# Two fused blocks on one core: four pieces of small work change their place around the last expert

## Chip, cores and metric

The kernel runs on one core of one Trainium2 chip. The metric is the device time of one execution in microseconds (us). Engines are named as in the profile: PE is TensorE (PEld its weight loads), DVE VectorE, ACT ScalarE, POOL GpSimd, SP SyncE. Each engine works through its own queue in order; semaphores let one wait for another.

## What is computed

Two blocks in a row on 512 tokens of width 1024. The first is differential attention, followed by a mixture of 16 experts in 4 groups, with two experts chosen for each token:

```python
h = silu(xt @ w_gate[e]) * (xt @ w_up[e])
h = h * combine[..., e]
y = y + h @ w_down[e]
```

The second block normalises the tokens and a context of 256 rows, shifts and scales both by factors made from a condition, projects them with one matrix, and mixes a Fourier branch with neighbourhood attention, in which every token also attends to the context:

```python
xn = _rms_norm(x, norm_g) * (1.0 + sc_x) + sh_x
cn = _rms_norm(ctx, norm_g) * (1.0 + sc_c) + sh_c
qx = _rms_norm(_heads(qx), q_norm_g)
kc = _rms_norm(_heads(kc), k_norm_g)
```

## The kernel before

Every float32 operand of a matmul is held as two float16 parts, high and low, and every product is three matmuls (`mm3`: high by high, high by low, low by high). `hilo` makes the parts: ACT writes the high one, DVE the low one. For a weight, `Weights.piece()` does this for 1024 of the 2048 columns of a buffer at a time; a weight matrix has four pieces. Its raw form is loaded by DMAs of 1 MB on SP's queue.

The experts come one after the other: `pick` gathers an expert's (up to 96) tokens by a one-hot matmul (`se`, `xgp`), `hidden` is the gate or up projection (bank `gu`), `silu` and `gated` make `hx` = silu(gate) * up, `down` is the projection back (bank `yp`), which ACT copies to `y` and POOL's queue stores to `y_d`. The one-hot matrices need each token's rank within its expert; the ranks come from router logits (`lgp`, `lgq`), a handful of tiny DVE operations (`ranks`, tile `misc_m`) and a counting matmul (`pk`).

Most of the program is ordered by a scheduler, which may move an instruction ahead of where it is written. From the last but one expert (`tail`, a manual schedule) to the second block's first projections the written order holds. The names of that stretch:

- `crow`, the two context row tiles (buffer `ctx`). Line 1101 takes their reciprocal norms (`row_rstd`: a Square with row sums on ACT, a tiny multiply-add on DVE, a power on POOL); line 1103 multiplies the rows by them on DVE.
- `W["k"]`, the key weights (raw `bk`, parts `bks`), and `W["v"]`, the value weights (`bv`, `bvs`). Before, one piece of the key weights stands behind the up projection of expert 15 and three behind the first two context columns.
- `spread` (line 1107 for the scale, `aB`; line 1243 for the shift, `bB`) spreads a row of factors over 128 partitions by 8 matmuls into each of two PSUM banks, which ACT copies to `AB`.
- After `down(15)` each engine reads a flag and may branch to a path for overfull experts (lines 1110 and 1111). Then `fetch` gathers each token's two expert rows from `y_d` by 8 indirect DMAs on POOL's queue (`yg`), `combined(t)` adds them to the token rows `XQ` by two DVE operations of 1024 columns for each of the four row tiles.
- `context_cols(k)` transposes 128 columns of the context on PE (`cnp`), and ACT and DVE make `cnT`; `project_c` projects keys (`kc`) and values (`vc`) of the context.
- `row_scale`, `row_affine`, `row_flip`: norm, scale and shift, transpose (`xnp`) of the four token row tiles. `row_affine` multiplies by scale and norm on DVE and adds the shift (line 1213), on POOL for row tiles 0 and 2 and on DVE for 1 and 3. The transposed rows `xnT` feed the keys `kx` (96 matmuls), and then `vx`, `qx` and `ng`, which PE runs one after the other.
- Lines 1289 to 1292 load the gains of the query and key norms (`g2rows`) over the router's weights in tile `sm` and multiply them by two DVE operations of 64 columns. They stand behind the manual schedule, so the scheduler places them.

Of the kernel before, what the change touches and what calls it, by code (L numbers as in the profile page):

```python
# [14 lines left out]
ALU = mybir.AluOpType  # L15
# [6 lines left out]
D = 1024  # L22
NT = 4
KD = 8
EPS = 1e-6
# [75 lines left out]
def block_kernel(ctx: ExitStack, tc: tile.TileContext, a, out, dbg=None):  # L101
    nc = tc.nc
# [100 lines left out]
    def rsqrt(ss, n, mult, eps, name):  # L203
        u = tiny.tile([P, n], F32, tag=f"rs{n}", name=name + "u")
        nc.vector.tensor_scalar(u, ss, mult, eps, op0=ALU.mult, op1=ALU.add)
        r = tiny.tile([P, n], F32, tag=f"rr{n}", name=name + "r")
        nc.gpsimd.tensor_tensor(r, u, mhalf[:, :n], op=ALU.pow)
        return r

    def row_rstd(src, name, scale=1.0):  # L210
        ss = tiny.tile([P, 1], F32, tag="ss", name=name + "ss")
        junk = sqt(name + "j").bitcast(F16)
        nc.scalar.activation(junk, src, AF.Square, accum_out=ss)
        return rsqrt(ss, 1, 1.0 / (D * scale * scale), EPS / (scale * scale), name)

    def transpose_to(o, in_, n=P):
# [147 lines left out]
    W = {}  # L364
# [604 lines left out]
    def hidden(e, j, nxt):  # L969
        wh, wl = EW[3 * e + j].w  # L970
        h, l = xgs[e]
        ps = bank("mm", f"gu{j}_{e}")
        for m in range(4):
            ms = slice(m * P, (m + 1) * P)
            o = ps[:, m * CAP:(m + 1) * CAP]
            for k in range(KD):
                mm(o, wh[:, k, ms], h[:, k, :], k == 0, False)
                mm(o, wh[:, k, ms], l[:, k, :], False, False)
                mm(o, wl[:, k, ms], h[:, k, :], False, k == KD - 1)
            if nxt:  # L980
                nxt.piece()
        psg[e, j] = ps
# [6 lines left out]
    def gated(e):  # L989
        sg = ht[e]  # L990
        stt(sg[:, :W4], psg[e, 1][:, :W4], DG * HS, sg[:, :W4], op1=ALU.mult)
        hx = h15(f"hx{e}")
        hilo(hx[:, :W4], hx[:, W4:], sg[:, :W4])
        ht[e] = hx
# [86 lines left out]
    e = NE - 2  # L1081
# [6 lines left out]
    crow, AB = ([x[:, i * D:(i + 1) * D] for i in range(2)] for x in (slot("ctx"), slot("AB")))  # L1088
    for t in range(2):
        nc.sync.dma_start(crow[t], a["ctx"][t * P:(t + 1) * P, :])  # L1090
    gated(e)
    e = NE - 1
    hidden(e, 0, EW[3 * e + 1])
# [4 lines left out]
    XP = rows("XQ")  # L1098
    for t in range(NT):
        nc.sync.dma_start(XP[:, t, :], x1_d[t * P:(t + 1) * P, :])  # L1100
    crs = [row_rstd(crow[t], f"cn{t}") for t in range(2)]
    for t in range(2):
        nc.vector.tensor_scalar(crow[t], crow[t], crs[t], None, op0=ALU.mult)
    hidden(e, 1, None)
    W["k"].piece(1)
    gated(e)
    run_all(spread(lambda k: aff[:, 0, k:k + 1], AB[0], "aB"))
    down(e, None)

    most = nc.values_load(flag[0:1, 0:1], min_val=0, max_val=2 * T)  # L1110
    with tc.If(most > CAP):
# [98 lines left out]
    def row_affine(t):  # L1210
        x = w4(f"xr{t}")
        stt(x, XP[:, t, :], rr[t], AB[0], op1=ALU.mult)
        (nc.gpsimd if t in (0, 2) else nc.vector).tensor_tensor(x, x, AB[1], op=ALU.add)
        xr[t] = x

    def row_flip(t):
# [22 lines left out]
        fetch(t)  # L1239
    context_cols(0)  # L1240
    context_cols(1)
    W["k"].piece(3)
    run_all(spread(lambda k: mod[:, k, 0:1], AB[1], "bB"))
    for k in range(KD):
        for t in range(2):
# [30 lines left out]
    for t, f in enumerate(kcn):  # L1276
        turn(f, cnat[:, t * 512:(t + 1) * 512], csp[:, t * 1024:(t + 1) * 1024],
             kvc16[:, :2048].rearrange("p (m t) -> p m t", m=8)[:, :, t * P:(t + 1) * P])()
    maskb = const.tile([P, 1152], F32, tag="misc", name="misc_b")
    mask = maskb[:, :768]  # L1280
    nc.sync.dma_start(mask, a["mask"])
# [4 lines left out]
    load_bias(0)  # L1286
    tail.close()

    nc.gpsimd.dma_start(S("wr", 0, 128), a["g2rows"])
    g2r = S("wr", 0, 64)  # L1290
    nc.vector.tensor_tensor(g2r, g2r, S("wr", 64, 64), op=ALU.mult)
    nc.vector.tensor_scalar(g2r, g2r, 4.0, None, op0=ALU.mult)
    gxc = const.tile([P, KD], F32, name="gxc")
    nc.vector.tensor_scalar(gxc, mod[:, 16:24, 0], 1.0 / (4.0 * SW), None, op0=ALU.mult)
    nc.gpsimd.dma_start(gx_d[0, :].rearrange("(k p) -> p k", p=P), gxc)
# [321 lines left out]
```

## Time and profile before

| | us |
|---|---|
| median of three runs | 856.88 |
| lowest, highest | 855.62, 859.67 |
| the profiled execution | 857.49 |
| span of its profile | 855.7 |

| engine | busy us | share of the span |
|---|---|---|
| PE | 788.8 | 92% |
| PEld | 495.6 | 58% |
| DVE | 642.0 | 75% |
| ACT | 522.0 | 61% |
| POOL | 148.7 | 17% |

Times below are counted from the start of the span; the profiled execution is 1.8 us longer than its span. The router stands at 270 to 300 us, the experts at 295 to 577, the context's projections at 577 to 606, the token rows and their keys at 594 to 636; from there to 699 PE runs without a gap. PE's clock has two levels, 2.4 GHz (1.00 in the profile) and 1.2 GHz (0.50); the mean granted was 0.979.

### The profile page before, as it was taken

The numbers are of one execution on the slowest core, as the hardware profiler recorded it, in microseconds if no ns is written. First come the engines' busy times: TensorE is split into PE (matmuls) and PEld (weight loads), VectorE is DVE, ScalarE is ACT, GpSimd is POOL, SyncE is SP. The second block draws the span as 40 slices with busy tenths as digits, with TensorE's granted clock in tenths as the row PEclk, the third lists the DMA queues.
The fourth block names the chain that finished last, engine by engine and source line by source line (L and its number), as shares of the span: only waits on it lengthen the run. The fifth ranks groups of instructions, "written<-read, shape, count | busy, mean of one in ns | idle before, by whom it ended". The sixth has DMA issues, their size and how long they took to land. (4 is left out here: it accounts for less than half of the span.)

```text
span 855.7 us, 18940 instructions
## 1 busy us (share of the span) xinstructions
PE 788.8 (92%) x7898; PEld 495.6 (58%) x7898; DVE 642.0 (75%) x1114; ACT 522.0 (61%) x847; POOL 148.7 (17%) x132
## 2 busy tenths in 40 slices
PE   5999999898989889999999999988899999899598
PEld 3445445454446588888888787754444445645344
DVE  4756658578985688999999999957955638986642
ACT  5635346455854378888887888767434347789400
POOL 1140121110053310000000000005550313231000
PEclk9999999999999799999999999999999999999899
DMA  9944201594163959999999999956554129696912
GB/s 339 388 169 148 99 1 26 161 266 164 50 242 128 333 193 350 393 394 398 395 395 396 397 395 394 367 194 230 189 164 138 30 57 199 137 200 126 252 59 68
DMA packets 127257, 192.91 MB, mean 225 GB/s; under 512 B 56271, under 2 KB 56784, under 8 KB 127168
## 3 DMA queue, kind: packets, MB, share of 16 engines
q1 hardware_dynamic: 121184, 172.33, 60.6%
q0 software_dynamic: 3776, 13.05, 4.2%
q10 hardware_dynamic: 2208, 6.29, 1.9%
q8 instruction: 63, 1.03, 0.5%
q14 instruction: 26, 0.21, 0.1%
HBM read 165.95 MB, written 12.59 MB: 209 GB/s over the span
## 5 line engine op out<-in xcount | busy, mean ns | idle before, releaser
L155 PEld LDWEIGHTS <-hT 128*128 128x128 f16 x576 | 55.8, 100 | 66.9 <-issue 9.9
L155 PEld LDWEIGHTS <-xnT 128*128 128x128 f16 x456 | 44.5, 99 | 53.6 <-issue 2.4
L155 PEld LDWEIGHTS <-hx 128*96 128x96 f16 x384 | 46.5, 125 | 39.7 <-ACT hx L166 5.5
L525 ACT ACTIVATE z<-z,mx 128x128 f32<-128x128 f32 (+3 forms) x64 | 35.4, 555 | 37.0 <-DVE mx L523 34.4
L1009 POOL DMA_DIRECT2D y_d<-y x16 | 8.2, 513 | 256.5 <-ACT y L1008 245.4
L155 PE MATMUL xgp<-se,XSh 128*128 128x96 f16 x512 | 48.3, 211 | 0.9 <-DVE se L940 0.9
L155 PE MATMUL xgp<-se,XSl 128*128 128x96 f16 x512 | 48.3, 211 | 0.0
L155 PEld LDWEIGHTS <-XSl 128*128 128x128 f16 x512 | 45.6, 101 | 1.0 <-issue 1.0
L155 PEld LDWEIGHTS <-XSh 128*128 128x128 f16 x512 | 45.6, 101 | 0.7 <-issue 0.7
L155 PEld LDWEIGHTS <-cT 128*128 128x128 f16 x216 | 20.4, 101 | 23.5 <-issue 4.3
L523 DVE CUSTOM_DVE_ANT_0 z<-s,misc_a 128x128 f32<-128x128 f32 (+3 forms) x64 | 29.8, 483 | 5.1 <-PE s L155 5.1
L1481 POOL TENSOR_TENSOR late_b<-late_b,misc_b 128x256 f32<-128x256 f32 x24 | 19.1, 818 | 78.8 <-DVE mxn L1484 74.6
L163 DVE SCALAR_TENSOR_TENSOR ring<-zn,ring 128x512 f16<-128x512 f32 x32 | 21.7, 699 | 13.7 <-ACT ring L1487 13.7
L155 PEld LDWEIGHTS <-oT 128*128 128x128 f16 x192 | 17.4, 99 | 20.8 <-issue 4.1
L1486 ACT ACTIVATE zn<-zn,mxn 128x512 f32<-128x512 f32 x32 | 22.8, 714 | 10.5 <-DVE mxn L1484 10.3
L155 PE MATMUL y<-wo0s,oT 128*128 128x512 f16 x96 | 26.5, 381 | 1.4 <-DVE on L577 1.2
L1484 DVE CUSTOM_DVE_ANT_0 zn<-ns,late_b 128x512 f32<-128x512 f32 x32 | 20.8, 679 | 8.1 <-PE ns L155 8.1
L155 PE MATMUL y<-wo1s,oT 128*128 128x512 f16 x96 | 23.9, 390 | 3.0 <-DVE XP L163 2.2
L1008 ACT ACTIVATE y<-yp 96x512 f32<-96x512 f32 x32 | 18.7, 586 | 9.1 <-PE yp L155 9.1
L155 PE MATMUL s<-kk,qk 64*128 64x128 f16 (+3 forms) x192 | 24.0, 302 | 0.2 <-DVE mx L523 0.2
L155 PE MATMUL v<-wv1s,hT 128*128 128x512 f16 x96 | 23.9, 399 | 0.0
L155 PE MATMUL z<-bo0s,cT 128*128 128x512 f16 x96 | 22.8, 384 | 1.1 <-DVE fg L163 1.1
(731 smaller groups left out, 2338.9 us busy)
## 6 DMA issues: line engine op xcount, KB each, us to landing
w_gate<-in_w_gate SPq DMA_DIRECT2D x32, 1024.0 KB, 13.2
w_up<-in_w_up SPq DMA_DIRECT2D x32, 1024.0 KB, 13.2
w_down<-in_w_down SPq DMA_DIRECT2D x32, 1024.0 KB, 13.5
ada<-in_w_ada SPq DMA_DIRECT2D x12, 1024.0 KB, 7.0
y_d<-y POOLq DMA_DIRECT2D x16, 384.0 KB, 7.2
wk<-in_da_w_in SPq DMA_DIRECT2D x4, 1024.0 KB, 13.5
wv<-in_da_w_in SPq DMA_DIRECT2D x4, 1024.0 KB, 10.8
wo<-in_da_w_out SPq DMA_DIRECT2D x4, 1024.0 KB, 10.2
```

The lines of the kernel that those rows point to most:

```text
L155: nc.tensor.matmul(o, lhsT=lhsT, rhs=rhs, start=start, stop=stop)
L163: return nc.vector.scalar_tensor_tensor(o, in0, sc, in1, op0=op0, op1=op1)
L523: nc.vector.tensor_tensor_reduce(out=z[:, :n], in0=ps[:, :n], in1=master[:, 384 - P * i:], scale=-hsc, scalar=3e38, op0=ALU.add, op1=ALU.m ...
L525: nc.scalar.activation(z[:, :n], z[:, :n], AF.Exp, bias=mx, scale=-1.0, accum_out=sums[:, c, i:i + 1])
L1008: nc.scalar.activation(y[:CAP, cs], ps[:CAP, :], AF.Copy, scale=1.0 / (HS * SW))
L1009: nc.gpsimd.dma_start(y_d[e * CAP:(e + 1) * CAP, :], y[:CAP, :])
L1481: nc.gpsimd.tensor_tensor(m[:, :256], pos[j, "b"][:, c * 256:(c + 1) * 256], mask[:, v:v + 256], op=ALU.add)
L1484: nc.vector.tensor_tensor_reduce(out=z, in0=st[j, t][c], in1=m, scale=-ISC, scalar=3e38, op0=ALU.add, op1=ALU.min, accum_out=mx)
L1486: nc.scalar.activation(z, z, AF.Exp, bias=mx, scale=-1.0, accum_out=sums[:, 2 * t + c:2 * t + c + 1])
```

## The change

Five edits, all of them of order or of engine; the arithmetic is the same.

1. The gating of expert 15 (`gated(e)`) stands ahead of the tiny operations and multiplies of the context's norm, of which only the two Squares on ACT (`row_squares`) stay ahead of it.
2. The key weights' four pieces all stand around and within `down(15)`: one ahead of it, two behind its first bank's matmuls, one behind its second's. Before, `down(15)` had none.
3. The shift of all four row tiles is added by DVE.
4. The load of the gains stands behind the context's load on SP's queue, in place of POOL's.
5. Their two multiplies stand at the end of the manual schedule, behind the norms of the context's keys.

```diff
--- before.py
+++ after.py
@@ -207,10 +207,14 @@
         nc.gpsimd.tensor_tensor(r, u, mhalf[:, :n], op=ALU.pow)
         return r
 
-    def row_rstd(src, name, scale=1.0):
+    def row_squares(src, name):
         ss = tiny.tile([P, 1], F32, tag="ss", name=name + "ss")
         junk = sqt(name + "j").bitcast(F16)
         nc.scalar.activation(junk, src, AF.Square, accum_out=ss)
+        return ss
+
+    def row_rstd(src, name, scale=1.0):
+        ss = row_squares(src, name)
         return rsqrt(ss, 1, 1.0 / (D * scale * scale), EPS / (scale * scale), name)
 
     def transpose_to(o, in_, n=P):
@@ -1088,6 +1092,7 @@
     crow, AB = ([x[:, i * D:(i + 1) * D] for i in range(2)] for x in (slot("ctx"), slot("AB")))
     for t in range(2):
         nc.sync.dma_start(crow[t], a["ctx"][t * P:(t + 1) * P, :])
+    nc.sync.dma_start(S("wr", 0, 128), a["g2rows"])
     gated(e)
     e = NE - 1
     hidden(e, 0, EW[3 * e + 1])
@@ -1098,14 +1103,15 @@
     XP = rows("XQ")
     for t in range(NT):
         nc.sync.dma_start(XP[:, t, :], x1_d[t * P:(t + 1) * P, :])
-    crs = [row_rstd(crow[t], f"cn{t}") for t in range(2)]
+    css = [row_squares(crow[t], f"cn{t}") for t in range(2)]
+    hidden(e, 1, None)
+    gated(e)
+    crs = [rsqrt(css[t], 1, 1.0 / D, EPS, f"cn{t}") for t in range(2)]
     for t in range(2):
         nc.vector.tensor_scalar(crow[t], crow[t], crs[t], None, op0=ALU.mult)
-    hidden(e, 1, None)
+    run_all(spread(lambda k: aff[:, 0, k:k + 1], AB[0], "aB"))
     W["k"].piece(1)
-    gated(e)
-    run_all(spread(lambda k: aff[:, 0, k:k + 1], AB[0], "aB"))
-    down(e, None)
+    down(e, W["k"])
 
     most = nc.values_load(flag[0:1, 0:1], min_val=0, max_val=2 * T)
     with tc.If(most > CAP):
@@ -1210,7 +1216,7 @@
     def row_affine(t):
         x = w4(f"xr{t}")
         stt(x, XP[:, t, :], rr[t], AB[0], op1=ALU.mult)
-        (nc.gpsimd if t in (0, 2) else nc.vector).tensor_tensor(x, x, AB[1], op=ALU.add)
+        nc.vector.tensor_tensor(x, x, AB[1], op=ALU.add)
         xr[t] = x
 
     def row_flip(t):
@@ -1239,7 +1245,6 @@
         fetch(t)
     context_cols(0)
     context_cols(1)
-    W["k"].piece(3)
     run_all(spread(lambda k: mod[:, k, 0:1], AB[1], "bB"))
     for k in range(KD):
         for t in range(2):
@@ -1276,6 +1281,9 @@
     for t, f in enumerate(kcn):
         turn(f, cnat[:, t * 512:(t + 1) * 512], csp[:, t * 1024:(t + 1) * 1024],
              kvc16[:, :2048].rearrange("p (m t) -> p m t", m=8)[:, :, t * P:(t + 1) * P])()
+    g2r = S("wr", 0, 64)
+    nc.vector.tensor_tensor(g2r, g2r, S("wr", 64, 64), op=ALU.mult)
+    nc.vector.tensor_scalar(g2r, g2r, 4.0, None, op0=ALU.mult)
     maskb = const.tile([P, 1152], F32, tag="misc", name="misc_b")
     mask = maskb[:, :768]
     nc.sync.dma_start(mask, a["mask"])
@@ -1286,10 +1294,6 @@
     load_bias(0)
     tail.close()
 
-    nc.gpsimd.dma_start(S("wr", 0, 128), a["g2rows"])
-    g2r = S("wr", 0, 64)
-    nc.vector.tensor_tensor(g2r, g2r, S("wr", 64, 64), op=ALU.mult)
-    nc.vector.tensor_scalar(g2r, g2r, 4.0, None, op0=ALU.mult)
     gxc = const.tile([P, KD], F32, name="gxc")
     nc.vector.tensor_scalar(gxc, mod[:, 16:24, 0], 1.0 / (4.0 * SW), None, op0=ALU.mult)
     nc.gpsimd.dma_start(gx_d[0, :].rearrange("(k p) -> p k", p=P), gxc)
```

The three stretches of the queues. First DVE's queue in the router, before: `lgq` is the last row tile's logits, `sm` the gains, `ge` to `misc_m` the ranks, `pk` the counts, `se` the first expert's one-hot matrix.

```order
L163 SCALAR_TENSOR_TENSOR misc_m<-lgq,m3r,sm 128x20
L1291 TENSOR_TENSOR sm<-sm 128x64
L873 TENSOR_TENSOR ge<-misc_m 128x80
L1292 TENSOR_SCALAR sm<-sm 128x64
L875 TENSOR_TENSOR ge<-ge,cst 128x80
L876 TENSOR_TENSOR df<-ge 128x20x4
L877 TENSOR_REDUCE misc_m<-df 128x20
L163 SCALAR_TENSOR_TENSOR misc_m<-misc_m 128x16
L163 SCALAR_TENSOR_TENSOR misc_m<-misc_m,pk 128x64
L940 TENSOR_TENSOR se_3084<-misc_m,cst 128x384
```

The same rows of the changed kernel:

```order
L163 SCALAR_TENSOR_TENSOR misc_m<-lgq,m3r,sm 128x20
L877 TENSOR_TENSOR ge<-misc_m 128x80
L879 TENSOR_TENSOR ge<-ge,cst 128x80
L880 TENSOR_TENSOR df<-ge 128x20x4
L881 TENSOR_REDUCE misc_m<-df 128x20
L163 SCALAR_TENSOR_TENSOR misc_m<-misc_m 128x16
L163 SCALAR_TENSOR_TENSOR misc_m<-misc_m,pk 128x64
L944 TENSOR_TENSOR se_3084<-misc_m,cst 128x384
```

The two operations on `sm` have left the router; in the changed kernel they stand far behind, between the sums of the token keys' norms.

DVE's queue ahead of expert 15's down projection, before (`sg` and `hx` are the gating, `cn0u`, `cn1u` and `ctx` the context's norm, `bks` the key weights):

```order
L163 SCALAR_TENSOR_TENSOR w_down15s_8486<-w_down_7995,w_down15s_8486 128x1024 x2
L205 TENSOR_SCALAR cn0u<-cn0ss 128x1
L205 TENSOR_SCALAR cn1u<-cn1ss 128x1
L1103 TENSOR_SCALAR ctx<-ctx,cn0r 128x1024
L1103 TENSOR_SCALAR ctx<-ctx,cn1r 128x1024
L163 SCALAR_TENSOR_TENSOR bks_8616<-bk_8449,bks_8616 128x1024
L163 SCALAR_TENSOR_TENSOR sg_8447<-gu_15_8519,sg_8447 128x384
L168 TENSOR_TENSOR hx_8620<-sg_8447,hx_8620 128x384
L1110 TENSOR_LOAD misc_m
```

And in the changed kernel:

```order
L163 SCALAR_TENSOR_TENSOR w_down15s_8487<-w_down_7995,w_down15s_8487 128x1024 x2
L163 SCALAR_TENSOR_TENSOR sg_8448<-gu_15_8510,sg_8448 128x384
L168 TENSOR_TENSOR hx_8608<-sg_8448,hx_8608 128x384
L205 TENSOR_SCALAR cn0u<-cn0ss 128x1
L205 TENSOR_SCALAR cn1u<-cn1ss 128x1
L1111 TENSOR_SCALAR ctx<-ctx,cn0r 128x1024
L1111 TENSOR_SCALAR ctx<-ctx,cn1r 128x1024
L163 SCALAR_TENSOR_TENSOR bks_8633<-bk_8450,bks_8633 128x1024 x2
L163 SCALAR_TENSOR_TENSOR bks_8652<-bk_8451,bks_8652 128x1024 x2
L1116 TENSOR_LOAD misc_m
```

The gating moved in front of the norm, and the four low parts of the key weights stand between the norm and the flag's load.

ACT's queue in the same place, before (`cn0j` and `cn1j` are the Squares, `AB` the spread scale, `y` the evacuations of the down projection):

```order
L213 ACTIVATE cn0j,cn0ss<-ctx 128x1024
L213 ACTIVATE cn1j,cn1ss<-ctx 128x1024
L166 ACTIVATE bks_8616<-bk_8449 128x1024
L166 ACTIVATE hx_8620<-sg_8447 128x384
L694 ACTIVATE AB<-aB_8623 128x512
L694 ACTIVATE AB<-aB_8629 128x512
L1008 ACTIVATE y_8635<-yp_8636 96x512
L1008 ACTIVATE y_8635<-yp_8650 96x512
L1110 TENSOR_LOAD misc_m
```

And in the changed kernel:

```order
L213 ACTIVATE cn0j,cn0ss<-ctx 128x1024
L213 ACTIVATE cn1j,cn1ss<-ctx 128x1024
L166 ACTIVATE hx_8608<-sg_8448 128x384
L698 ACTIVATE AB<-aB_8621 128x512
L698 ACTIVATE AB<-aB_8627 128x512
L166 ACTIVATE bks_8633<-bk_8450 128x1024 x2
L166 ACTIVATE bks_8652<-bk_8451 128x1024
L1012 ACTIVATE y_8636<-yp_8637 96x512
L166 ACTIVATE bks_8652<-bk_8451 128x1024
L1012 ACTIVATE y_8636<-yp_8656 96x512
L1116 TENSOR_LOAD misc_m
```

One key piece left its place ahead of `hx`; three stand ahead of the first evacuation and one ahead of the second. In the changed kernel none is left between the first context columns and the spread shift, where three stood.

The buffers that the pieces and the gathered rows use also change: the second half of the gathered rows (`yg` of row tiles 2 and 3) takes the two buffers of the raw key weights, where before it took buffers of expert 15's weights. PE's queue is the same up to the token keys, where the transposes of row tiles 2 and 3 stand a few matmuls later.

## Rows read from the trace of the kernel before

**Rows 1.** The page: busy time, share of the span and instructions of each engine.

```profile
PE 788.8 (92%) x7898; PEld 495.6 (58%) x7898; DVE 642.0 (75%) x1114; ACT 522.0 (61%) x847; POOL 148.7 (17%) x132
```

**Rows 2.** PE's waits, 276:318 (first row), 552:660: total us, times, longest.

```profile
PE pk L155 <- DVE misc_m L163: 2.6, 1, 2.6
...
PE yp L155 <- ACT hx L166: 5.1, 2, 3.7
PE kc L155 <- ACT AB L694: 2.8, 1, 2.8
PE xnp L217 <- DVE xnT L163: 2.5, 1, 2.5
```

**Rows 3.** Timeline, router: start, us, engine, line, tiles, count, [idle before <- releaser].

```profile
292.41 0.23 DVE L1291 TENSOR_TENSOR sm<-sm 128x64 f32<-128x64 f32 x1 [3.25 <-DMA sm<-in_g2rows]
...
289.22 2.04 PE L155 MATMUL modp<-cst,ar 128*128 128x2 f32 x16 [0.54 <-ACT ar L758]
```

**Rows 4.** Stretches: us, busy PE, PEld, DVE, ACT, POOL, clock, DMA share, GB/s.

```profile
290.00:292.00 2.00, 1.26 (x11) 1.20 (x11) 0.00 (x0) 1.06 (x2) 0.00 (x0) 0.73 1.02 406
...
296.00:298.00 2.00, 2.00 (x28) 2.00 (x26) 1.39 (x2) 0.08 (x1) 0.00 (x0) 0.50 1.05 388
...
300.00:302.00 2.00, 2.00 (x37) 2.00 (x35) 0.99 (x3) 1.52 (x3) 0.00 (x0) 0.71 1.04 385
...
315.00:320.00 5.00, 4.62 (x97) 4.04 (x94) 4.49 (x7) 1.98 (x3) 0.00 (x0) 1.00 0.20 21
...
570.00:577.50 7.50, 7.20 (x27) 3.56 (x26) 0.25 (x1) 1.74 (x4) 0.00 (x0) 0.77 0.02 5
```

**Rows 5.** Timeline, the last gating and its down projection: DVE, ACT, PE.

```profile
567.42 1.22 DVE L163 SCALAR_TENSOR_TENSOR bks<-bk,bks 128x1024 f16<-128x1024 f32 x1
568.55 0.55 DVE L163 SCALAR_TENSOR_TENSOR sg<-gu,sg 128x384 f32<-128x384 f32 x1
...
564.29 1.05 ACT L213 ACTIVATE cn1j<-ctx 128x1024 f16<-128x1024 f32 x1
...
569.14 0.52 ACT L166 ACTIVATE hx<-sg 128x384 f16<-128x384 f32 x1 [2.75 <-DVE sg L163]
...
539.36 5.34 PE L155 MATMUL yp<-w_down13s,hx 128*96 128x512 f16 x24
...
569.71 7.23 PE L155 MATMUL yp<-w_down15s,hx 128*96 128x512 f16 x24 [3.74 <-ACT hx L166]
```

**Rows 6.** Timeline, from the branch to the token keys: ACT, PE.

```profile
579.66 2.93 ACT L166 ACTIVATE bks<-bk 128x1024 f16<-128x1024 f32 x3
582.50 1.06 ACT L694 ACTIVATE AB<-bB 128x512 f32<-128x512 f32 x2
...
583.12 0.81 PE L155 MATMUL kc<-bks,cnT 128*128 128x512 f16 x3 [2.82 <-ACT AB L694]
...
621.04 15.49 PE L155 MATMUL kx<-bks,xnT 128*128 128x512 f16 x71
```

**Rows 7.** Timeline, the token rows: DVE, POOL.

```profile
594.41 5.12 DVE L163 SCALAR_TENSOR_TENSOR XQ<-yg,misc_m,XQ 128x1024 f32<-128x1024 f32 x4
...
603.27 4.56 DVE L163 SCALAR_TENSOR_TENSOR XQ<-yg,misc_m,XQ 128x1024 f32<-128x1024 f32 x2
...
609.12 1.23 DVE L1213 TENSOR_TENSOR xr<-xr,AB 128x1024 f32<-128x1024 f32 x1
...
613.91 2.69 DVE L163 SCALAR_TENSOR_TENSOR xr<-XQ,xn3r,AB 128x1024 f32<-128x1024 f32 x1
...
603.75 3.00 POOL L1213 TENSOR_TENSOR xr<-xr,AB 128x1024 f32<-128x1024 f32 x1
```

**Rows 8.** Timeline, POOL: the last store of expert rows and the last gather.

```profile
577.87 0.56 POOL L1009 DMA_DIRECT2D y_d<-y  x1 [11.15 <-ACTq L1111]
...
593.42 1.54 POOL L1172 DMA_INDIRECT yg<-y_d,misc_m  x1 [0.30 <-issue]
```

**Rows 9.** The gathered rows' tile: time from issue to landing.

```profile
DMA to landing us min/median/max: 5.3/5.7/6.2
```

## The prediction

> **What bounds the kernel now.** First the page: PE is busy for 92% of the span, no other engine for more than 75% [rows 1]. So the question for each edit is whether it removes time in which PE waits or runs slowly; an engine freed elsewhere gives nothing. Second, PE's waits in the two places that the change touches [rows 2]: 2.6 us in the router for the ranks of the last row tile, then 3.7 for expert 15's gating, 2.8 for the spread shift, 2.5 for the low parts of the first transposed token rows. Third, the timeline, for what made each of them late. In the router DVE stood 3.25 us before a tiny multiply of the norm gains, because their load had not landed; the ranks that PE waits for are queued behind it on DVE [rows 3]. Before the last down projection, the gating on DVE starts only behind the context's norm and a 1.22 us key piece [rows 5]. Before the context's keys, ACT makes three key pieces in 2.93 us and only then copies the spread shift, whose bank PE needs [rows 6]. Fourth, PE's clock in these stretches: 0.73, 0.50, 0.71 around the router's wait and 0.77 in the down projection behind the 3.7 us wait [rows 4]. That is the lower level, 1.2 GHz, in part of each; the engine had waited or done only tiny matmuls shortly before.
>
> After the token keys begin in earnest, at 621.04, 71 matmuls run in one piece [rows 6], and the projections behind them follow with no wait of PE. So a gain made ahead of 621 is kept if nothing later is tied to an earlier event; the loads of later weights are issued by the same queues and move along.
>
> **The change, part by part.** The sum is made against the profiled execution, 857.49 us; the median of the three runs is 0.6 lower.
>
> *Gains' multiplies out of the router.* DVE stops from 289.16 to 292.41 (3.25 us). Without the stop its remaining chain, from 292.41 to the count's start on PE at 291.26 + 2.64 = 293.90, takes 1.5 us and would be done at 290.7. But PE itself is busy until 289.22 + 2.04 = 291.26 [rows 3]. So PE's 2.6 us go [rows 2], not 3.25, and what is then late is PE's own queue. The first expert's gather follows directly. Is it kept through sixteen experts? Their weights come at 385 to 406 GB/s with the DMA engines full, but between 315 and 320 the share is 0.20 [rows 4]: there the loads wait for buffers, which DVE and PE release earlier too, and no engine's wait list between 320 and 553 holds a DMA. I take 2.6; the ends are 0 (given back to the loads) and 5.2 (with the clock, below). In their new place the two multiplies of 0.23 us each at most [rows 3] stand on DVE while PE runs 71 matmuls [rows 6]: nothing, or 0.5 if that cover were gone. Their load stands on SP's queue ahead of the key weights, 64 KB before loads of 1 MB each that are read 20 us later: nothing.
>
> *Gating first.* The second Square ends on ACT at 564.29 + 1.05 = 565.34; the gating product on DVE needs 0.55 and no longer waits for the norm, which itself waits for these Squares, so it is done by then. So `hx` starts at about 565.4 in place of 569.14, and PE, which still spreads the scale until 565.97 (569.71 - 3.74), goes on without a stop [rows 5]: 3.7 us. If ACT's Squares held `hx` longer than that it would be 3.2 to 3.7.
>
> *Clock.* The last down projection takes 7.23 us for 24 matmuls, expert 13's the same 24 in 5.34 [rows 5]; the difference stands behind the wait, and the level falls inside that stretch [rows 4]. With no wait ahead I take 1.9; the ends are 0 (the level falls there all the same) and 1.9.
>
> *Key pieces early.* The three pieces in front of the shift's copy go (2.93 us of ACT [rows 6]). In the new place they run during 5.3 us of down projection, three before the first evacuation and one between the two; that delays the first evacuation by 1 to 2 us but not the second, and only the second releases the store. On DVE four low parts of about 1.2 us [rows 5] run behind the gating and the norm: an estimate is 566.5 for the gating's end (565.4 + 0.52 + 0.55), 2.1 for the norm (from the second Square's end at 565.34 to 567.42, as before), 4 x 1.22 for the parts, so until 573.5; PE's down projection ends at 565.97 + 5.34 = 571.3, and transposes and ACT's two steps lie between it and DVE's first context part, so the last key part and DVE's branch may hold that by some tenths. Of the 2.8 us wait [rows 2] I take 2.6; ends 1.5 and 2.8.
>
> So keys of the context's second tile start at 583.1 - 3.7 - 1.9 - 2.6 = 574.9, 8.2 earlier. The loop behind it, ACT and PE in turn, is the same, and so are the 10 us of context values on PE.
>
> *Shift on DVE.* Two adds of 1.23 us come to DVE, +2.46. Beside POOL's adds two DVE operations were stretched: two sums took 4.56 where four took 5.12 (1.28 each), 2.0 too long, and one scale took 2.69 for 1.28, 1.4 too long [rows 7]. Sum on DVE: -0.9. The chain that ends last here is DVE to PE's transposes, and it also loses the POOL add that follows the third norm; POOL's add of 3.00 us [rows 7] becomes 1.23. I take 1.2 in all. The ends: +2.0, and -2.5 if the stretched ones come again without POOL (the DMA engines are full there too).
>
> *Gathers.* The sums wait for gathered rows. The last gather starts at 593.42 [rows 8] and lands 5.7 later [rows 9], at 599.1; the store they all wait for leaves at 577.87 [rows 8] and moves with the down projection by 5.6, so the last one lands at 593.5. The sums start 8.2 earlier, at 586.2 [rows 7], and come to the last row tile behind four sums (5.1), two sums (2.6), a scale (1.3) and the new add (1.2), at 596.4. Hidden, with 3 us to spare; the third tile's have about 1. The two buffers that gathers take over from the key weights are free when the fourth low part is done, at 573.5, ahead of the gathers.
>
> The sum: 2.6 + 3.7 + 1.9 + 2.6 + 1.2 = 12.0 us. 857.5 - 12.0 = 845.5; less the 0.6 by which the median lies lower, **845.0 us** (1.4% faster).
>
> **One rule against the rows.** The rows show PE at 0.50 from about 291 to 301 [rows 4], over the whole gather of the first expert, so this execution paid about 2.5 us for it: some 5 us of matmuls at half speed. The Trainium skill (TensorE: Matmul & The Clock Gate, "What's actually happening") says that the moment at which the level changes is free-running and differs from run to run. By the rows the level falls at the same point again, since PE's work ahead of 291 is unchanged, and the sum stays; by the rule the changed kernel can find this gather at the full clock in some executions. What this would give is the fourth rival's price.
>
> **The rivals.**
> 1. The router's 2.6 us are given back to the weights' loads: 847.6. For it, full DMA engines over some 210 us; against it, the 0.20 in between [rows 4] and no wait for a DMA.
> 2. DVE becomes the bound of the token rows, with its stretched operations back (-2.5 in place of +1.2): 848.7. For it, DMA traffic in the same stretch; against it, the stretched ones are just those beside POOL's adds [rows 7].
> 3. The change doesn't do what it says: `hx` stays late behind something on ACT or PE not shown, so that the 3.7 and 1.9 and the 2.6 behind them stay: 845.0 + 8.2 = 853.2.
> 4. The clock is at the full level for the first gather: 842.5.
> 5. Slower: PE still waits for DVE ahead of the token keys (2.5 us, [rows 2]) and falls to the lower level there, and the level does not come back. Every us of matmuls costs another one. To use up 12 us and make it 0.5% (4.3 us) slower, it would have to stay down for twice 16.3, about 33 us of these dense matmuls: 861.2 and more. The longest stretch at 0.50 before is 10 us, with PE idle in part of it [rows 4].
>
> **How the numbers follow.** Forecast 845.0, chance 0.58; rivals in order: 0.13 (847.6), 0.12 (848.7), 0.06 (853.2), 0.08 (842.5), 0.03 (861.2 or more). The range takes in the forecast with its bounds and rivals 1, 2 and 4: 842.0 to 849.5. Of the 0.91 of chance in these, about 0.1 is left out for errors of single terms. A measurement of this kernel can tell about 0.5% (4.3 us) from no change: faster is below 852.6. Forecast and rivals 1, 2, 4 lie below, 0.91; rival 3 within, 0.06; rival 5 above, 0.03.
>
> **What would show it.** Right: no DVE wait for the gains' load and no wait of PE for the count; `hx` under 1 us behind the second Square; the last down projection in 5.3 to 5.6 us right behind the spread; PE's wait for `AB` under 0.5; the four key pieces on ACT inside the down projection; sums of 1.28 us each and all four adds 1.2 on DVE; the 69 or so last key matmuls in one piece at about 609 (2.6 + 8.2 + 1.2 ahead of 621). Wrong: a new wait of ACT or DVE for a DMA in the experts (rival 1), sums that wait for `yg`, DVE operations of 2 us and more without POOL beside them (rival 2), or 0.50 in the clock over more than 10 us behind 599 (rival 5).

## The result and the profile after

The changed kernel takes 845.98 us in the median of four runs (843.73 to 847.60) against 856.25 us for the kernel before on the same chip (853.89 to 859.67): a ratio of 0.9873, 95% interval 0.9847 to 0.9899, so 1.3% faster. Two more sets of six runs gave 0.9873 (0.9841 to 0.9905) and 0.9874 (0.9844 to 0.9904). The forecast of 845.0 us and its range 842.0 to 849.5 held. Its terms did not all hold: the router brought more than forecast, the tail less, and one wait came that the forecast had counted as "some tenths".

The profiled execution took 846.84 us, its span 845.1. First the page's busy line, to be set beside [rows 1] (PE 92% there):

```profile
PE 787.7 (93%) x7898; PEld 496.3 (59%) x7898; DVE 641.6 (76%) x1116; ACT 522.5 (62%) x847; POOL 141.0 (17%) x129
```

PE's waits between 276 and 318 us (engine, tile and line, what was waited for, us in total, times, longest); the 2.6 for `misc_m` of [rows 2] is gone:

```profile
PE gu L155 <- DVE w_gate1s L163: 1.0, 1, 1.0
PE xgp L155 <- DVE se L944: 0.9, 1, 0.9
PE gu L155 <- issue: 0.8, 1, 0.8
PE modp L155 <- ACT ar L762: 0.5, 1, 0.5
```

PE's waits between 555 and 615 us. The waits for `hx` and for `AB` of [rows 2] are gone, the one for `xnT` is as it was (2.5 before), and one is new, for DVE's sequencer (DVEq) at line 1117, which is the `tc.If` on the flag:

```profile
PE xnp L221 <- DVE xnT L163: 2.8, 1, 2.8
PE cnp L221 <- DVEq L1117: 2.1, 1, 2.1
PE kx L155 <- ACT xnT L166: 0.3, 1, 0.3
```

The timeline of the last expert's end: ACT, PE and DVE (start, duration, engine, line, what, in brackets the idle time before it):

```profile
560.67 0.53 ACT L166 ACTIVATE hx<-sg 128x384 f16<-128x384 f32 x1
...
561.25 5.54 PE L155 MATMUL yp<-w_down15s,hx 128*96 128x512 f16 x24
...
564.09 4.62 DVE L163 SCALAR_TENSOR_TENSOR bks<-bk,bks 128x1024 f16<-128x1024 f32 x4
...
568.92 0.63 PE L221 MATMUL cnp<-cst,ctx 128*128 128x128 f32 x4 [2.13 <-DVEq L1117]
569.39 2.88 PE L155 MATMUL bB<-cst,mod 128*128 128x128 f32 x16
```

The rows that answer to [rows 5] are as forecast: `hx` directly behind the second Square, no stop of PE, the down projection in 5.54 us in place of 7.23. Then PE stops. The rows of the context that it is to transpose were ready at 564.2, when DVE's scale of them ended; but DVE goes on to four low parts of key pieces until 568.71, and only behind them passes the branch that PE's transposes stand behind. After this stop the clock falls. Stretches of the trace (length, busy time of PE, PEld, DVE, ACT and POOL with counts, PE's granted clock, DMA share, GB/s):

```profile
290.00:298.00 8.00, 7.09 (x105) 7.02 (x105) 4.58 (x8) 1.99 (x4) 0.00 (x0) 0.57 1.04 395
570.00:576.00 6.00, 6.00 (x29) 3.99 (x29) 1.26 (x3) 3.80 (x8) 2.86 (x3) 0.72 0.31 88
600.00:606.00 6.00, 5.32 (x24) 3.35 (x25) 5.96 (x9) 2.12 (x5) 1.46 (x1) 0.72 0.37 140
```

A mean of 0.72 over 6 us is 1.7 us of full speed lost (6 x 0.28), the same as at 570 to 576 before, where it lay in the down projection. The spread `bB` shows it: 2.88 us for 16 matmuls that took 1.95 before.

Last, DVE's row stage, which answers to [rows 7]; every pair of sums takes 2.6 us, where one pair took 4.56:

```profile
584.78 5.12 DVE L163 SCALAR_TENSOR_TENSOR XQ<-yg,misc_m,XQ 128x1024 f32<-128x1024 f32 x4
...
593.76 1.23 DVE L1219 TENSOR_TENSOR xr<-xr,AB 128x1024 f32<-128x1024 f32 x1
594.91 2.60 DVE L163 SCALAR_TENSOR_TENSOR XQ<-yg,misc_m,XQ 128x1024 f32<-128x1024 f32 x2
...
606.38 1.22 DVE L1219 TENSOR_TENSOR xr<-xr,AB 128x1024 f32<-128x1024 f32 x1
```

To place each microsecond, the span is cut at four events that all kernels below have: the first `modp` matmul in the router, expert 0's gating on DVE (`sg`), the spread scale `aB`, the context's values `vc`, and the end of the last run of token key matmuls `kx`. Lengths in us, each a difference of two starts (or of a start and an end) in the traces:

| kernel | modp to sg 0 | to aB | to vc | to kx end |
|---|---|---|---|---|
| before | 28.2 | 246.5 | 31.5 | 41.1 |
| changed, three traces | 25.0, 25.0, 25.1 | 246.2 | 26.5, 27.2, 26.5 | 39.9, 39.5, 39.7 |
| e1_gains (gains alone) | 25.0 | 246.2 | 31.5 | 41.1 |
| e2_gating (gating alone) | 28.3 | 246.2 | 27.3 | 41.5 |
| e3b_pieces_back (all but pieces) | 25.1 | 246.2 | 27.4 | 39.3 |
| e4_shift_back (all but shift) | 25.2 | 246.2 | 26.6 | 41.5 |
| e5_lows_later | 25.0 | 246.2 | 27.1 | 39.5 |
| e6_branch_late | 25.0 | 246.2 | 30.4 | 39.7 |
| e7_lows_once | 25.2 | 246.2 | 23.2 | 41.2 |
| e8_rows_order, e8b | 23.9, 25.0 | 246.2 | 23.1, 23.4 | 38.5, 38.5 |

Of the 10.6 us between the first two spans, 3.2 lie in the router, 0.3 in the experts, 5.0 in the last expert and context, 1.2 in the row stage, 1.1 ahead of the router, and -0.2 behind the keys. That last 1.1 is none of the change's: `modp` starts at 289.22 in the kernel before, at 288.12, 289.18 and 289.17 in the three traces of the changed one. From `modp` to the end of `kx` the three are 9.5 to 9.8 us shorter than the kernel before. What follows, which the change leaves alone, takes 219.2 us before and 219.4, 216.7 and 216.9 in the three; this part differs from execution to execution by more than some of the terms below.

### The profile page after: what moved, and what is told of

Its sections match the earlier page's. It is cut to its first block, busy times and chain, and to the rows that moved or that the text cites. A ratio compares the mean times of both kernels' runs of the same rounds, so it can differ in the third digit from the quotient of the medians.

```text
span 845.1 us, 18940 instructions
## 1 busy us (share of the span) xinstructions
PE 787.7 (93%) x7898; PEld 496.3 (59%) x7898; DVE 641.6 (76%) x1116; ACT 522.5 (62%) x847; POOL 141.0 (17%) x129
## 5 line engine op out<-in xcount | busy, mean ns | idle before, releaser
L1490 ACT ACTIVATE zn<-zn,mxn 128x512 f32<-128x512 f32 x32 | 22.9, 715 | 10.4 <-DVE mxn L1488 10.3
L155 PE MATMUL y<-wo0s,oT 128*128 128x512 f16 x96 | 27.1, 388 | 1.2 <-DVE on L581 1.2
L155 PE MATMUL y<-wo1s,oT 128*128 128x512 f16 x96 | 23.9, 390 | 3.0 <-DVE XP L163 2.2
L155 PE MATMUL k<-wk1s,hT 128*128 128x512 f16 x96 | 22.5, 379 | 0.9 <-DVE k1nat L300 0.9
L166 ACT ACTIVATE pth<-pt 128x128 f16<-128x128 f32 (+3 forms) x32 | 13.8, 431 | 15.1 <-PE pt L221 15.0
```

The source lines that it names most:

```text
L155: nc.tensor.matmul(o, lhsT=lhsT, rhs=rhs, start=start, stop=stop)
L166: nc.scalar.activation(h, src, AF.Copy, scale=scale)
L1490: nc.scalar.activation(z, z, AF.Exp, bias=mx, scale=-1.0, accum_out=sums[:, 2 * t + c:2 * t + c + 1])
```

## The experiments

My theory after the first trace: the gain is the router's wait, the gating and part of the clock; the early key pieces exchanged PE's wait for `AB` for one on DVE's branch, and so brought next to nothing. The rivals: the router's gain is given back to the loads; the pieces brought their 2.6 us all the same; the new wait is covered by what follows.

**The gains alone** (e1_gains). The kernel before with

```diff
@@ in the last two experts
+    nc.sync.dma_start(S("wr", 0, 128), a["g2rows"])
@@ behind the keys' turn
+    g2r = S("wr", 0, 64)
+    nc.vector.tensor_tensor(g2r, g2r, S("wr", 64, 64), op=ALU.mult)
+    nc.vector.tensor_scalar(g2r, g2r, 4.0, None, op0=ALU.mult)
@@ behind tail.close()
-    nc.gpsimd.dma_start(S("wr", 0, 128), a["g2rows"])
-    g2r = S("wr", 0, 64)
-    nc.vector.tensor_tensor(g2r, g2r, S("wr", 64, 64), op=ALU.mult)
-    nc.vector.tensor_scalar(g2r, g2r, 4.0, None, op0=ALU.mult)
```

> The kernel before with only the move of the norm gains (load on SP ahead of the last expert, the two multiplies behind the keys' turn). My theory: DVE's 3.25 us stop and PE's 2.6 us wait for the ranks are gone, the gain is kept through the sixteen experts: 2.6 to 3.0 us off, 856.3 to 853.5, ratio 0.9965 to 0.997; expert 0's gating (sg) and expert 14's then come earlier by the same number; the later waits (hx 5.1, kc 2.8) stay as before. Rival: the gain is given back to the weights' loads, ratio 1.000, sg of expert 14 no earlier than in the kernel before although sg of expert 0 is.

Measured: 853.28 us against 856.79, ratio 0.9965 (0.9939 to 0.9991). The stretch from `modp` to the gating of expert 0 fell from 28.2 to 25.0 us, and the next one, through fifteen experts to `aB`, did not grow (246.5 to 246.2). The count follows `modp` with no wait:

```profile
290.06 1.95 PE L155 MATMUL modp<-cst,ar 128*128 128x2 f32 x16 [0.54 <-ACT ar L758]
291.87 0.17 PE L155 MATMUL pk<-misc_m,tri 128*128 128x16 f16 x1
```

So the loads give nothing back: the rival is out, and the term is 3.2 us. The sign that the prediction named for it, a wait for a DMA in the experts, does come now and then (0.4 us once on DVE in the first trace of the changed kernel, 0.4 twice in the third, none in the second), but the stretch takes 246.2 us in all three.

**The gating alone** (e2_gating). The kernel before with the following (the definition of `row_squares`, the same as in the change, is left out here)

```diff
-    crs = [row_rstd(crow[t], f"cn{t}") for t in range(2)]
-    for t in range(2):
-        nc.vector.tensor_scalar(crow[t], crow[t], crs[t], None, op0=ALU.mult)
+    css = [row_squares(crow[t], f"cn{t}") for t in range(2)]
     hidden(e, 1, None)
-    W["k"].piece(1)
     gated(e)
+    crs = [rsqrt(css[t], 1, 1.0 / D, EPS, f"cn{t}") for t in range(2)]
+    for t in range(2):
+        nc.vector.tensor_scalar(crow[t], crow[t], crs[t], None, op0=ALU.mult)
     run_all(spread(lambda k: aff[:, 0, k:k + 1], AB[0], "aB"))
+    W["k"].piece(1)
     down(e, None)
```

> The kernel before with only expert 15's gating moved ahead of the context's norm (the first key piece stands behind the gating, the other three at their old place). My theory: hx follows the second Square by under 1 us, PE's 3.7 us wait is gone and the last down projection takes 5.3 to 5.6 us instead of 7.2; nothing behind it takes that back, so 5.4 us off: 850.9, ratio 0.9937. Rival: the row stage is held by gathered rows or by POOL's adds and gives part back: 3 us off or less, 853.3, ratio 0.9965.

Measured: 848.82 us against 856.79, ratio 0.9913 (0.9880 to 0.9946), more than I expected but with 5.4 us (0.9937) inside. The traced execution is the slowest of the six, 853.64 us at a mean clock of 0.975 (the fastest took 847.56 at 0.986), so what follows is one execution with much of the lower clock, and no trace shows the others. It says where the 5.6 us of wait and clock go. From `aB` to `bB` it is 13.75 us before and 8.24 here, all of it. But from `aB` to `vc` only 4.2 us are left, because the clock, which no longer falls in the down projection, falls behind the next wait:

```profile
571.56 1.95 PE L155 MATMUL bB<-cst,mod 128*128 128x128 f32 x16
...
576.98 1.21 PE L155 MATMUL kc<-bks,cnT 128*128 128x512 f16 x3 [2.82 <-ACT AB L698]
```

```profile
564.00:576.00 12.00, 9.86 (x59) 6.49 (x59) 6.01 (x11) 8.54 (x15) 1.94 (x3) 1.00 0.31 103
576.00:582.00 6.00, 5.02 (x18) 2.44 (x18) 3.74 (x4) 4.07 (x8) 4.97 (x4) 0.72 0.52 152
```

In the kernel before the same wait for `AB` (2.82 us, until 583.12) had no fall behind it; there the clock had fallen ahead of it, in the down projection:

```profile
570.00:576.00 6.00, 6.00 (x21) 2.98 (x20) 0.25 (x1) 1.22 (x3) 0.00 (x0) 0.72 0.02 4
...
582.00:588.00 6.00, 4.79 (x24) 2.37 (x24) 4.21 (x5) 5.31 (x10) 4.83 (x4) 1.00 0.52 139
```

So in this execution the clock term moved by one wait, and most of it (5.5 - 4.2 = 1.3) was paid there.

**The key pieces put back** (e3_pieces_back, and again e3b_pieces_back for a trace beside more times). The changed kernel with

```diff
-    down(e, W["k"])
+    down(e, None)
     ...
     context_cols(1)
+    W["k"].piece(3)
```

> The changed kernel with three of the four key pieces back behind the context's first columns. My theory from the trace of after: the early pieces removed PE's 2.8 us wait for the spread shift but put a 2.1 us wait and about 1.3 us at the lower clock on PE instead, ahead of DVE's branch, so they brought nothing: within 0.8 us of the changed kernel, 845.2 to 846.8, ratio 0.987 to 0.989. The wait cnp<-DVEq is under 0.5 us here and kc<-ACT AB 2 to 3 us. Rival (the prediction's term): the early pieces brought 2.6 us: 848.6, ratio 0.991.

> The changed kernel with three of the four key pieces at their old place behind the context's first columns, once more, for a second trace and more times. From the other traces: the stretch from the spread scale (aB) to the context's values takes 27.3 us with the pieces there (as in the kernel with the gating alone) and 26.5 with them early, so 0.8 us slower than the changed kernel, ratio 0.988; the prediction's term would be 2.6 us, ratio 0.990.

Measured: 848.38 us, ratio 0.9883 (0.9842 to 0.9924), and 849.66 us, ratio 0.9894 (0.9858 to 0.9929). In us both lie above the 845.2 to 846.8 of my theory, and the first is the rival's number; but the kernel before is slower on these chips too (856.79 and 858.72), so the ratios count. In the trace of e3b_pieces_back the waits are exchanged, as the theory has it:

```profile
PE kc L155 <- ACT AB L698: 2.7, 1, 2.7
PE cnp L221 <- PEq L1117: 0.5, 1, 0.5
```

From `aB` to the end of `kx` it is 66.6 us here and 66.4, 66.7 and 66.2 in the changed kernel: 0.2 us of difference on average. But this sum isn't taken at the same clock. In the row stage the clock does not fall here, although PE waits for `xnT` as long as in the changed kernel (which has a mean of 0.72 in these 6 us):

```profile
600.00:606.00 6.00, 4.15 (x25) 2.53 (x26) 5.96 (x9) 2.25 (x5) 1.45 (x1) 1.00 0.49 188
...
601.34 1.25 PE L221 MATMUL xnp<-cst,xr 128*128 128x128 f32 x8 [2.84 <-DVE xnT L163]
```

From `aB` to `vc`, where this trace and the three of the changed kernel each lose 1.7 us of full speed, it is 27.4 us here and 26.5, 27.2 and 26.5 there: the pieces are worth 0.2 to 0.9. By the ratios it is 0.9 to 1.8 us (0.10 to 0.21% of 856), with intervals that reach from below nothing to over 2.6. That the waits are exchanged is shown; the size is not settled, 0.2 to 1.8 us.

**The shift put back** (e4_shift_back). The changed kernel with

```diff
-        nc.vector.tensor_tensor(x, x, AB[1], op=ALU.add)
+        (nc.gpsimd if t in (0, 2) else nc.vector).tensor_tensor(x, x, AB[1], op=ALU.add)
```

> The changed kernel with the shift's adds for row tiles 0 and 2 back on POOL. My theory: the stretched DVE operations come back (two sums in 4.5 us, a scale in 2.6), and the transposes of the token rows come 1.2 us later: 847.2, ratio 0.9895. Rival: the row stage is set by PE's context values and DVE's last low parts alone, nothing changes: 846.0, ratio 0.988. Second rival: DVE is the bound of the stage and is relieved by two adds: 844, ratio 0.9855.

Measured: 846.97 us, ratio 0.9889 (0.9857 to 0.9920); the time alone can't tell 1.2 us. The trace can: beside POOL's add two sums take 4.57 us again. From the first sum to the shift of the last row tile DVE's chain takes 22.5 us here (606.95 - 584.49) and 21.6 in the changed kernel (606.38 - 584.78). Within 0.02 us, three more traces with adds on POOL have the first number (the kernel before, e1_gains, e2_gating), and four without have the second (e3b_pieces_back, e6_branch_late, the two others of the changed kernel). So the shift is worth 0.86 us on DVE. The stretch from `vc` to the end of `kx` is 41.5 us in place of 39.5 to 39.9, but 3.4 us of full speed are lost in it against 1.7 (in the kernel before it is 41.1 with 1.7 lost): what goes beyond 0.86 lies in the part of PE's work in which the clock falls, and whether the adds caused it isn't shown.

```profile
584.49 5.12 DVE L163 SCALAR_TENSOR_TENSOR XQ<-yg,misc_m,XQ 128x1024 f32<-128x1024 f32 x4
...
593.35 4.57 DVE L163 SCALAR_TENSOR_TENSOR XQ<-yg,misc_m,XQ 128x1024 f32<-128x1024 f32 x2
...
593.83 3.01 POOL L1219 TENSOR_TENSOR xr<-xr,AB 128x1024 f32<-128x1024 f32 x1
...
604.33 2.36 DVE L163 SCALAR_TENSOR_TENSOR xr<-XQ,xn3r,AB 128x1024 f32<-128x1024 f32 x1
...
606.95 1.21 DVE L1219 TENSOR_TENSOR xr<-xr,AB 128x1024 f32<-128x1024 f32 x1
```

**The branch later** (e6_branch_late, beside the changed kernel once more, a2_changed). The changed kernel with

```diff
     down(e, W["k"])
+    for i in (2, 3):
+        f, c = i // 2, slice(i % 2 * 1024, i % 2 * 1024 + 1024)
+        stt(W["k"].s[f][:, 1, c], W["k"].r[f][:, c], SW, W["k"].s[f][:, 0, c], op1=ALU.subtract)
```

> The changed kernel with the low parts of the last two key pieces computed twice on DVE ahead of its branch (the same values are written again, 2 x 1.16 us more of DVE, nothing else). My theory: PE's wait cnp<-DVEq grows by as much, from 2.1 to 4.4 us, and the end moves by 2.3 us or more: 848.3 to 849.5, ratio 0.990 to 0.9915. Rival: the wait is covered by what comes behind it (gathered rows that the sums wait for): cnp waits longer, the end moves by under 0.7 us: 846.3, ratio 0.988. Second rival: PE waits there for something other than DVE's queue: the wait stays 2.1 us.

> The changed kernel once more, beside the two others, for its spread and for a second trace. Expected: 846 us, 0.9873 of the kernel before; the same waits of PE (cnp<-DVEq 2.1, xnp<-DVE xnT 2.5 to 2.9, none for the ranks, hx or AB); the stretch from the router's first tiny matmuls (modp) to expert 0's gating 25.0 us as in the first trace (28.2 in the kernel before); the lower clock behind the count and behind the cnp wait again.

Measured: 849.42 us (0.9904, 0.9870 to 0.9938) against 846.03 for the changed kernel on the same chip. PE's wait grew by 2.27 us for two low parts:

```profile
572.17 1.08 PE L221 MATMUL cnp<-cst,ctx 128*128 128x128 f32 x4 [4.40 <-DVEq L1120]
```

The stretch from `aB` to `vc` grew by 3.2 to 3.9 us, more than the wait, since the clock stays low for longer (a mean of 0.57 over 570 to 578). What DVE has queued ahead of its branch is paid by PE one for one, and nothing behind covers it. Both rivals are out.

**The low parts later** (e5_lows_later, then e7_lows_once). The first attempt took three low parts away from the branch. `high` and `low` are the two steps of a piece, on ACT and on DVE (their definitions are left out here):

```diff
@@ in down(e, nxt, high=None), ahead of the copy of each half
+            if high:
+                for i in high[c]:
+                    W["k"].high(i)
     ...
-    down(e, W["k"])
+    down(e, None, ((1, 2), (3,)))
     ...
     context_cols(1)
+    W["k"].low(1)
     ...
+        if k in (0, 1):
+            W["k"].low(k + 2)
```

> The changed kernel with the low parts (DVE) of the last three key pieces behind DVE's branch: one behind the context's first two columns, one each in the first two steps of the key loop; their high parts stay on ACT inside the last down projection. My theory: in the changed kernel PE's first transposes of the context stand behind DVE's branch, and that behind four low parts; with one low part ahead of the branch PE's wait cnp<-DVEq falls from 2.1 us to under 0.5, no wait for AB comes back, and the context's values start 2.1 to 3.4 us earlier (3.4 if the stretch at the lower clock behind that wait goes too): 842.5 to 844, ratio 0.9835 to 0.985. Rival: the row stage is tied to the gathered rows, or the later low parts make PE wait for bks or DVE start its sums no earlier: within 0.6 us of the changed kernel, 846, ratio 0.988.

Measured: 846.18 us, ratio 0.9894 (0.9856 to 0.9932): no gain. The wait for the branch was gone and the clock did not fall there, but PE waited in the key loop:

```profile
PE kc L155 <- DVE cnT L163: 2.4, 3, 1.2
PE kc L155 <- ACT cnT L166: 1.4, 2, 0.7
```

The cause was my edit. The accessor `.w` of the weights makes every piece that its count says is missing, and as I had left the count, the key loop's first use made pieces 2 and 3 in full, beside the parts that the edit places, and ahead of the next columns of the context:

```profile
571.15 2.36 DVE L163 SCALAR_TENSOR_TENSOR bks<-bk,bks 128x1024 f16<-128x1024 f32 x2 [0.36 <-ACT bks L166]
```

So this run is no answer to its question. e7_lows_once makes each part once (`half(i, True)` is the low part, and the count goes on with the high parts), with one more low part ahead of the branch, where DVE has time, and two behind the first two columns (left out here: the definition of `half`, and the loop in `down` that makes the high parts with it):

```diff
-    down(e, W["k"])
+    down(e, None, ((1, 2), (3,)))
+    W["k"].half(1, True)
     ...
     context_cols(1)
+    for i in (2, 3):
+        W["k"].half(i, True)
     run_all(spread(lambda k: mod[:, k, 0:1], AB[1], "bB"))
```

> The changed kernel with the low parts of the key's last two pieces (DVE) moved from ahead of DVE's branch to behind the context's first two columns, ahead of the spread shift; the low part of the second piece stays ahead of the branch, the high parts of all stay on ACT inside the last down projection. No piece is made twice, as two were in the run called e5_lows_later, which so had 2.4 us more of DVE and 2 us of ACT in front of the context's columns. My theory: the wait cnp<-DVEq falls from 2.1 us to under 0.5, DVE has 3 us free where the two low parts now stand, and the context's values start 2.1 us earlier, or 3.6 if the lower clock behind that wait goes too: 842.4 to 844, ratio 0.983 to 0.985. Rival: PE's gain is taken back in the row stage, by gathered rows or by the next wait with its own lower clock: within 0.7 us of the changed kernel, ratio 0.9875.

Measured: 844.93 us, ratio 0.9848 (0.9812 to 0.9883). Neither wait is there, the clock is whole in this part, and `aB` to `vc` takes 23.2 us, 3.3 less than the changed kernel's best:

```profile
PE xnp L221 <- DVE xnT L163: 2.9, 1, 2.9
PE cnp L221 <- PEq L1131: 0.5, 1, 0.5
```

```profile
568.00:580.00 12.00, 11.82 (x66) 6.32 (x65) 8.89 (x13) 10.96 (x21) 6.66 (x5) 1.00 0.56 162
596.00:604.00 8.00, 6.87 (x26) 4.32 (x27) 7.97 (x12) 2.40 (x5) 1.46 (x1) 0.57 0.48 186
```

But the row stage takes 41.2 us where it took 39.5 to 39.9: the next wait, for `xnT`, is followed by 8 us at a mean of 0.57, twice the loss of before (3.4 us against 1.7). Theory and rival were both half right: the wait's own time is kept, the clock's part is given back at the next wait.

**The next wait too** (e8_rows_order, and e8b_rows_order beside the changed kernel, a3_changed). The second row tile's transposes need a PSUM bank that DVE frees only behind the fourth tile's sums. e7_lows_once with

```diff
     row_affine(0)
-    combined(3)
     row_scale(2)
     row_affine(1)
     ...
     row_flip(0)
+    combined(3)
     row_scale(3)
```

> The kernel of e7_lows_once with one more thing moved: the fourth row tile's sums on DVE stand behind the transposes of the first row tile and the second tile's scale and shift, in place of ahead of them. My theory: the second tile's transposes wait 2.8 us for a PSUM bank that DVE frees only behind those sums (xnp<-DVE xnT); that wait falls to under 0.7 us, and with it 1 to 2.5 us of the end: 840 to 842.5, ratio 0.981 to 0.984. Rival: DVE is busy in one piece through the row stage, so the last tile's transposes and the end come no earlier: the same as e7_lows_once within 0.7 us.

> The kernel of e8_rows_order once more, beside the changed kernel on one chip. My theory: it is 4 to 5 us faster than the changed kernel (841 to 842 where that takes 846): 3.3 us from the context part, where neither the wait for DVE's branch nor the lower clock behind it comes back, and 1 to 2 us in the row stage, where the second tile's transposes no longer wait 2.8 us. Rival: the first figure, 841.3, rested on runs with little of the lower clock; then the two are within 2.5 us, and the trace has the lower clock again in the row stage (0.50 somewhere between 560 and 610).

> The changed kernel beside e8b_rows_order on one chip: 846 us, with the wait cnp<-DVEq of 2.1 us and the lower clock behind it, and xnp<-DVE xnT of 2.5 to 2.9 us.

Measured: 841.33 us, ratio 0.9814 (0.9773 to 0.9855), and the second time 839.63 us (838.40 to 842.06), ratio 0.9823 (0.9796 to 0.9850), against 844.83 us (841.11 to 847.13) for the changed kernel on that chip: 5.2 us less. This beats both kernels. Of the 5.6 us between the two spans of that chip, 3.1 lie between `aB` and `vc` and 1.2 between `vc` and the end of `kx`; another 1.3 lie ahead of the router, where the two kernels do the same. PE's longest wait in this part is 1.2 us now, and in both traces the clock does not fall at all from 560 to 612 (here the second):

```profile
PE xnp L221 <- DVE xnT L163: 1.5, 2, 1.2
PE cnp L221 <- PEq L1131: 0.7, 1, 0.7
```

```profile
560.00:590.00 30.00, 28.95 (x150) 15.03 (x149) 23.12 (x31) 21.88 (x38) 15.19 (x14) 1.00 0.60 193
590.00:612.00 22.00, 20.26 (x107) 10.63 (x106) 20.54 (x31) 9.30 (x20) 6.81 (x5) 1.00 0.46 180
```

## Why the prediction was right, and where it was not

*Router: 2.6 forecast, 3.2 measured.* The mechanism held, and rival 1 (given back to the loads) is refuted by e1_gains. The wait itself was 2.6; with what it pushed, 2.9 lie between `modp` and the last count (4.68 us before, 1.81 after) and 0.4 behind it. I had not taken the upper end, and rightly: the clock falls at 290 in all three traces of the changed kernel (a mean of 0.57 over 290 to 298 in each), so rival 4 did not come. (The first trace of e8_rows_order took 23.9 us there where all others with the gains moved took 25.0 to 25.2; that much of it can come.) In another place the fall does stand elsewhere from trace to trace: the changed kernel has it at 194 to 200 in its first trace and at 164 to 170 in its second. The Trainium skill (TensorE: Matmul & The Clock Gate, "What's actually happening") says that the point at which the level changes varies from run to run. Here the traces agree with it (the first trace's rows, then the second's):

```profile
164.00:170.00 6.00, 6.00 (x38) 3.05 (x37) 3.28 (x10) 3.36 (x8) 0.00 (x0) 1.00 1.04 366
194.00:200.00 6.00, 5.68 (x28) 2.01 (x29) 4.63 (x20) 3.44 (x12) 0.00 (x0) 0.72 0.95 361
```

```profile
164.00:170.00 6.00, 6.00 (x31) 2.84 (x30) 2.68 (x9) 2.52 (x7) 0.00 (x0) 0.72 0.97 337
194.00:200.00 6.00, 3.64 (x22) 1.37 (x23) 4.29 (x18) 3.09 (x11) 1.01 (x1) 1.00 1.05 397
```

*Gating first: 3.7 forecast, 3.8 measured* (`aB` to the down projection: 5.75 us before, 1.95 after). Right; rival 3 is out.

*Clock: 1.9 forecast, 1.7 measured in the down projection, and 1.3 to 1.7 given back.* The step that failed: "with no wait ahead I take 1.9", with the end 0 only for a fall "there all the same". It fell not there but behind the next wait, `AB` in e2_gating, the branch in the changed kernel. From `aB` to `vc` 1.7 us of full speed are lost before and after alike.

*Key pieces early: 2.6 forecast, 0.2 to 1.8 measured* (0.2 to 0.9 by the stretch, 0.9 to 1.8 by the times). This is the step that was wrong. The prediction had both numbers: DVE's low parts until 573.5, PE's down projection until 571.3, so DVE 2.2 us late. It then argued that PE's transposes "lie between", as if they could start without DVE, and left "some tenths". They can't: their wait stands behind DVE's branch, and the 2.2 us stood in full (2.13). Both rates show it is the branch: two more low parts ahead of it, 2.27 us more of wait; two fewer, and the wait is gone.

*Shift on DVE: 1.2 forecast, 0.86 measured on DVE's chain*, where the prediction's own sum for DVE was 0.9; the stretch from `vc` to the end of `kx` differs by 1.2 to 2.0 us, with more of the lower clock at the upper end, and what makes the rest isn't shown. The stretched sums came back with POOL's adds in e4_shift_back (4.57 us) and are gone without them (2.60), so rival 2 is out. The ground that was given for it, full DMA engines there too, holds at most for the stretched sums of the kernel before; the stretched scale at 613.91 [rows 7] ran with the DMA engines idle (the share is the last but one number, 0.00):

```profile
606.00:612.00 6.00, 2.48 (x16) 1.77 (x17) 5.97 (x8) 2.42 (x5) 2.46 (x3) 0.98 0.96 373
612.00:618.00 6.00, 5.88 (x25) 2.86 (x24) 6.00 (x7) 3.36 (x8) 3.52 (x2) 0.73 0.00 1
```

The gathers stayed hidden: no sum waits for `yg`.

*Sum.* From `aB` on the forecast had 9.4 us and the traces have 6.2; the router and experts had 2.6 and brought 3.6; and 1.1 us in this pair of traces are variation ahead of the router. The last 69 key matmuls start at 610.65, where the forecast said about 609. The medians differ by 10.3 us. So the total of 12.0 was 1.7 us too high by the medians, and 2.2 to 2.5 by the stretches from `modp` to the end of `kx`. The forecast of 845.0 (its sum gives 844.9) still came within 1.0 us, for two reasons that are luck: the router's surplus stood against the tail's shortfall, and the median of the kernel before came out at 856.25, 0.6 below the 856.88 from which the forecast started. Rival 5 was far off: behind the wait ahead of the token keys 1.7 us of full speed are lost (a mean of 0.72 over 600 to 606), not 16.

## What to carry to other kernels

Before work is moved ahead of a conditional, write down for each engine when it reaches the branch: if another engine's first work behind it waits for that engine, the latest sets the start, whatever data is ready. Move only the part that fits (here the high parts on ACT and two low parts on DVE), and put the rest behind the first short work after the branch. And count a clock gain only where no other stop of PE follows: here the clock stayed up through the whole stretch only in the two traces in which the stops for `hx`, for `AB` and for the branch were gone and the one for `xnT` was down to 1.2 us.

## What the runs showed of the hardware that I had not expected

The fall of TensorE's clock moved along with the waits. With the wait for `hx` gone it fell behind the wait for `AB` (2.8 us, which before had no fall behind it); with that gone, behind the branch (2.1 us); with that gone, for longer behind the wait for `xnT` (2.9 us); and with that at 1.2 us it did not fall. Not every wait of this length had a fall behind it: in e3b_pieces_back one of 2.8 us for `xnT` had none. Where a fall followed, 1.7 or 3.4 us of full speed were lost, and not all of that reached the end: 1.3 us did in e2_gating, while the row stage, where PE waits for DVE's chain, takes 39.3 us without a fall (e3b_pieces_back) and 39.5 to 39.9 with one (the changed kernel).

Much of the spread between executions of one kernel goes with the granted clock: the six of e8_rows_order run from 837.95 us at a mean clock of 0.990 to 845.59 us at 0.978. A term of 1 us, as that of the shift, does not stand out of this in six runs, while two fixed events on DVE showed it in all nine traces compared (0.86 us).
